# Second FFN of a two-layer decoder: the sums of x one product earlier, the third pair's products woven into the end of the first two, and another place for the shorter split distance

## The chip, the cores and the metric

One core of one Trainium2 chip runs the whole program. The metric is the device time in microseconds (us) of one execution; the comparison below goes by the median of several runs. All matrix products are done in fp32r (a 32-bit format that TensorE takes), with each operand split in two: a high part (a rounded copy, made by ScalarE) and a low part (the operand minus its high part, made by VectorE). A product of two split operands takes three matmuls: high by high, high by low, low by high.

## The reference

```python
def _swiglu(x, w_gate, w_up, w_down):
    return (jax.nn.silu(x @ w_gate) * (x @ w_up)) @ w_down

def reference(x, ...):
    for i in range(DEPTH):                       # DEPTH = 2
        if i % N_MIXERS == 0:
            h = _multiscale_pool(x, pool_w[j], pool_scale[j])
        else:
            h = _diff_attention(x, w_qkv[j], w_o[j], lam_p[j], subln_g[j], rel_table, lambda_init)
        x = _layernorm(ALPHA * x + h, ln_mix_g[i], ln_mix_b[i])
        x = _layernorm(ALPHA * x + _swiglu(x, w_gate[i], w_up[i], w_down[i]), ln_ffn_g[i], ln_ffn_b[i])
    return x
```

x is 512 tokens by 1024 features; the hidden width of the FFN is 2816. The change touches only the FFN of the second layer (i = 1), and there only its opening: the first of the products with `w_gate` and `w_up`.

## The kernel before

The program is one instruction stream per engine, in the order in which the Python code issues it; each engine works through its own list in order, and semaphores make an instruction wait for its inputs. So the place of a line in the Python loop decides what stands in front of it on its engine.

**Seven products for eight.** Gate and up products of the FFN are computed with a scheme of the Strassen kind: for each index k of 0 to 10 (a pair of hidden blocks) seven products named P1, Q5, P6, Q3, P7, P2 and Q4 replace eight. Each is a run of 24 matmuls of 128x256 (`run`, line 966). P1, P2 and Q4 multiply quarters of x itself; Q5, P6, P7 and Q3 multiply sums of quarters of x, which are kept in `xs[:, m]` with m = 0, 1, 2, 3 in that order. P1, P6, P7 of one k add up in a PSUM bank called A, P2 in B, Q4 in D, Q5 and Q3 in C. In the middle of an accumulation the bank is copied out and then added to further: after P6 of a k, ScalarE copies bank A to `first` (line 985), and P7 of the same k, which adds to bank A, has to wait for that copy. In the same way Q5 is copied out of bank C (line 983) before Q3 adds to it.

**The opening order.** In the second layer the 21 products of k = 0, 1, 2 are run in the order of the list `FIRST`. In this text product j is the one at place j in that list, and chunk j is the piece of weights that it multiplies; chunk j has the names w108 to w111 for j = 0 to 3 and g_4, g_5, ... for j = 4, 5, ... in the trace, with h and l for the high and the low part. Before the change the order is

- j = 0 to 5: P1, P2 of k = 0, 1, 2; j = 6, 7, 8: Q4 of k = 0, 1, 2
- j = 9, 10: Q5 of k = 0, 1; j = 11, 12: P6; j = 13, 14: P7; j = 15, 16: Q3 of k = 0, 1
- j = 17, 18, 19, 20: Q5, P6, P7, Q3 of k = 2.

From j = 21 on come the seven products of k = 3, then of k = 4, and so on.

**Weights.** A chunk is loaded by SyncE's queue into one of five `raw` buffers (512 KB each); the load of chunk c waits until the low part of chunk c - 5 has been made, since that frees the buffer. ScalarE casts the chunk to its high part (line 711), VectorE makes the low part (line 714). There are six pairs of split buffers. `advance(upto)` issues casts and lows until the chunks below `upto` are complete; a cast of chunk c + 1 stands ahead of the low of chunk c. `ahead(j + 6)` after product j therefore issues the cast of chunk j + 6 and the low of chunk j + 5; `ahead(j + 5)` is one chunk less. From chunk 22 on, weights of k = 3 are partly sums of raw pieces that VectorE adds (line 708).

**Sums of x.** `sums_of_x` is a generator. In the second layer it has seven steps, and the loop issues one step per product (`next(sums)`). With r0 to r3 the four quarters of x, low and high being the split of a sum into `xs`:

- step 1: r1 = r0 - r1 (line 766); step 2: high of `xs[0]`, r0 = r2 - r0 (769); step 3: low of `xs[0]`, r2 = r1 - r2 (772); step 4: high of `xs[1]`, r3 = r3 + r2 (775)
- step 5: low of `xs[1]`, high of `xs[2]`; step 6: low of `xs[2]`, high of `xs[3]`; step 7: low of `xs[3]`.

The highs are casts of 128x1024 on ScalarE (line 751), the rest is VectorE (the lows are line 754).

**What else stands in the lists.** After j = 3, 5 and 7 a gate sum (lines 1026 and 1027) copies bank A of k = 0, 1, 2 and adds bank B. After each Q4, ScalarE copies bank D (line 998). After P7, VectorE and ScalarE compute the second half of the hidden block (lines 989, 1001, 1002, 1003), after Q3 the first half (lines 987, 1017). At the same time GpSimd's queue moves weight sums through DRAM (`tsum`), with DMAs that wait only for each other.

Of the kernel before, what the change touches and what calls it, by code (L numbers as in the profile page):

```python
# [52 lines left out]
GATE = ("P1", "Q5", "P6", "Q3", "P7", "P2", "Q4")  # L53
FIRST = [(k, p) for k in range(3) for p in ("P1", "P2")]
FIRST += [(k, "Q4") for k in range(3)]
FIRST += [(k, p) for ks in ((0, 1), (2,)) for p in ("Q5", "P6", "P7", "Q3") for k in ks]
PAIRS = [(0, 2), (2, 2), (4, 2), (6, 2), (8, 2), (10, 1)]


# [1 line left out]
def trunk(ctx, tc, x, wall, pscale, lam_p, subln, table, lng, lnb, first, onehot, out):  # L61
# [6 lines left out]
    def bank(name):  # L68
        return ps.tile([P, 512], F32, tag="bank", name=name)
# [523 lines left out]
    def ffn(layer, late):  # L593
# [8 lines left out]
        with tc.tile_pool(name=f"ffn{layer}", bufs=1) as fp:  # L602
# [118 lines left out]
            def ahead(upto):  # L721
                advance(upto)
                if upto > len(chunks):
                    prepare(upto - len(chunks), upto - len(chunks))
# [181 lines left out]
            def prepare(upto, lefts):  # L906
                while prepared[0] < min(upto, len(items)):
                    refill()
                    split_item(prepared[0])
                    held[0] -= 1  # L910
                    prepared[0] += 1
                while prepared[1] < min(lefts, len(items)):
                    left(prepared[1])
                    prepared[1] += 1
# [14 lines left out]
            def strassen(k):  # L929
                first_pairs = early_sums and k < 3  # L930
# [15 lines left out]
                def both(t):  # L946
                    return t.rearrange("p (f t) -> p f t", f=2)

                def tile_of(i):
                    if first_pairs and i == 0:  # L950
                        return hid[:, (6, 7, 17)[k], :]
                    return keep.tile([P, S], F32, tag="y", name=f"sg{layer}_{k}_{i}", bufs=2)

                def run(p):
                    j = place[k, p]
                    if names[p] not in banks:
                        banks[names[p]] = bank(f"{names[p]}{layer}_{k}")
                    acc = banks[names[p]]
                    h, l = halves[j]
                    xh, xl = lefts[p]  # L960
                    for f in range(2):
                        o = acc[:, f * 256 : (f + 1) * 256]
                        for kk in range(4):
                            c = slice((4 * f + kk) * P, (4 * f + kk + 1) * P)
                            for e, (w, x) in enumerate(((h, xh), (h, xl), (l, xh))):
                                nc.tensor.matmul(  # L966
                                    o, w[:, c], x[:, kk, :],
                                    start=(p in opening and not (onto and p == "P2")) and f + kk + e == 0,
                                    stop=p in closing and (f, kk, e) == (1, 3, 2),
                                    skip_group_check=True,  # L970
                                )
                    acc = both(acc)
                    if first_pairs and p in ("P1", "P2"):
                        return
                    g1 = None
                    if p == "P1" and onto:
                        banks["B"] = bank(f"B{layer}_{k}")
                        nc.scalar.copy(banks["B"], banks["A"])
                    elif p == "P1":
                        tiles[0] = tile_of(0)  # L980
                        nc.scalar.copy(both(tiles[0]), acc)
                    elif p == "Q5":
                        nc.scalar.copy(second, acc)  # L983
                    elif p == "P6":
                        nc.scalar.copy(first, acc)  # L985
                    elif p == "Q3":
                        tt(first, acc, first, op=ALU.subtract)  # L987
                    elif p == "P7":
                        tt(second, second, acc, op=ALU.subtract)
                    elif p == "P2":  # L990
                        if not onto:
                            tt(both(tiles[0]), acc, both(tiles[0]), op=ALU.add)
                    elif not first_pairs:
                        g1 = tile_of(1)
                        nc.scalar.activation(both(g1), acc, AF.Silu)  # L995
                    elif first_pairs:
                        tiles[1] = hid[:, (18, 8, 19)[k], :]
                        nc.scalar.copy(both(tiles[1]), acc)
                    if first_pairs and p == "P7":
                        g1 = tile_of(1)  # L1000
                        tt(both(g1), acc, both(tiles[1]), op=ALU.add)
                        nc.scalar.activation(g1, g1, AF.Silu)
                        tt(second, both(g1), second, op=ALU.mult)
                    if j >= early:
                        ahead(j + (5 if first_pairs and j >= 17 else 6))
                        if not (early_sums and p == "P7"):
                            catch_up()
                        if early_sums and j > 9:
                            next(chain, None)
                    if not early_sums and k == split_pairs[0] and p == "P1":  # L1010
                        weight_sums()
                    if p == "P2":
                        if onto:
                            tiles[0] = tile_of(0)
                        nc.scalar.activation(tiles[0], banks["B"] if onto else tiles[0], AF.Silu)
                    elif p == ("Q3" if first_pairs else "Q4"):
                        tt(first, both(tiles[0]), first, op=ALU.mult)
                        if not first_pairs:
                            tt(second, both(g1), second, op=ALU.mult)
                        if not early_sums and k < HALF - 1:  # L1020
                            weight_sums()
                        (owing if early_sums else behind).append(sum_hidden(k))
# [13 lines left out]
            sums = sums_of_x()  # L1036
            if early_sums:
                for i in range(2):
                    saved[1, i] = spare(4 + 11 * i)
                chain = in_pairs([down_sums(i) for i in range(AHEAD, len(PAIRS))])  # L1040
                runs = [strassen(k) for k in range(3)]
                gate_sums_after = (3, 5, 7)
                for j, (k, p) in enumerate(FIRST):
                    runs[k][0](p)
                    if j < 2:
                        advance(5 + j, True)
                        late[0, j]()
                    if j == 1:
                        nc.scalar.preload_act_table_set("silu_and_others")
                    if 2 <= j < early:  # L1050
                        advance(j + 5, True)
                    if 2 < j < 10:
                        next(sums)
                    if j in gate_sums_after:
                        runs[gate_sums_after.index(j)][1]()
                    if p == "P6":
                        runs[k][2]()
            else:
                accs = [(bank(f"g{layer}_{f}"), bank(f"u{layer}_{f}")) for f in range(early)]
                load_terms(0)  # L1060
                load_terms(1)
                for lo in (0, 256):
                    for f in range(early):
                        for i in range(2):
                            product(accs[f][i], 2 * f + i, lo, lo + 256)
                            if not lo and (f, i) in late:
                                late[f, i]()
                            if not lo and f + i:
                                advance(6, True)
                                next(sums, None)  # L1070
                        if lo:
                            advance(2 * f + 6)
                            gated(order[f], *accs[f])
                            catch_up()
                            next(sums, None)
                            if f < 2:
                                weight_sums()
                            if f == 1:
                                behind.append(sum_hidden(0))
                plain(early)  # L1080
# [66 lines left out]
            for p in DOWN:  # L1147
# [5 lines left out]
                for i in range(together):  # L1153
                    j = j0 + i
# [652 lines left out]
```

## Time and profile before

| | us |
|---|---|
| median of 3 runs | 931.76 (931.69 to 931.82) |
| the profiled execution, its own time | 931.79 |
| its span, first to last instruction | 930.0 |
| TensorE busy (PE) | 919.2 (99%) |
| VectorE busy (DVE) | 812.1 (87%) |
| ScalarE busy (ACT) | 522.7 (56%) |
| GpSimd busy (POOL) | 151.1 (16%) |

The time of the profiled execution exceeds its span by 1.8 us, which lie around the program. PEld is the loading of weights into TensorE, which overlaps PE; SPq is SyncE's queue of DMA issues. Rows of the order-of-time view give start, duration, engine, line, operation, out<-in, shapes and count, and in brackets how long the engine was idle before and what ended that. Matmuls overlap in time: each row lasts longer than the distance to the next. All starts are microseconds from the start of the span. The opening of the second FFN runs from 591 to 656.

### The profile page before, as it was taken

The page shows a single profiled execution, that of the slowest core. Times are in us where ns is not written, and L with a number is a line of the kernel's source. Part 1 is how long each engine was busy: PE and PEld are TensorE (multiplying, and loading weights), DVE is VectorE, ACT ScalarE, POOL GpSimd, SP SyncE. Part 2 cuts the span into 40 slices and gives each one's busy share as a digit, 9 for nine tenths or more (in the row PEclk, how much of TensorE's full clock was granted, in tenths as well). Part 3 has the DMA queues.
Part 4 walks back from the last instruction along what each step waited for, and adds up shares of the span by engine and source line. Part 5 has one row for each costly group of instructions (what it writes and reads, how often), then busy time and mean ns, then how long its engine had stood idle before and what let it go on. Part 6 is the DMA issues. An engine that isn't in the chain of part 4 may idle for free.

```text
span 930.0 us, 16198 instructions
## 1 busy us (share of the span) xinstructions
PE 919.2 (99%) x6285; PEld 850.3 (91%) x6285; DVE 812.1 (87%) x1199; ACT 522.7 (56%) x849; POOL 151.1 (16%) x203
## 2 busy tenths in 40 slices
PE   9999999999999999999999999999999999999996
PEld 8999999999988888988888888999999999988885
DVE  7999999998978798788787898888899999987687
ACT  5744555554653467565556675885555544654470
POOL 2311121110001101432423233222000000001100
PEclk9999999999999999999999999999999999999998
DMA  7388898896877965998999879999344644577952
GB/s 277 120 249 268 286 282 253 264 289 193 257 241 245 374 210 165 297 265 227 272 243 244 196 247 291 271 336 302 99 140 156 207 134 137 154 252 253 372 180 90
DMA packets 77962, 217.08 MB, mean 233 GB/s; under 512 B 7732, under 2 KB 19188, under 8 KB 77342
## 3 DMA queue, kind: packets, MB, share of 16 engines
q1 hardware_dynamic: 37660, 122.16, 38.8%
q0 software_dynamic: 22576, 70.79, 30.2%
q10 hardware_dynamic: 17650, 23.10, 6.9%
q8 instruction: 49, 0.80, 0.3%
q14 instruction: 27, 0.22, 0.1%
HBM read 190.84 MB, written 67.13 MB: 277 GB/s over the span
## 4 chain that ended last, share of the span: by engine, by line
PE 89%; DVE 4%; ACT 3%; issue 1%; DMA 1%; SPq 0%; POOL 0%; DVEq 0%; POOLq 0%; ACTq 0%
PE A L966 23%; PE P L1116 16%; PE C L966 12%; PE Q L1116 6%; PE B L966 5%; PE s L1385 2%; PE v L149 2%; PE v L150 2%; PE v L151 2%; PE k L149 2%; PE k L151 2%; PE q L149 2%; PE k L150 2%; PE q L150 2%; PE q L151 2%
## 5 line engine op out<-in xcount | busy, mean ns | idle before, releaser
L708 DVE TENSOR_TENSOR raw<-raw,raw 128x1024 f32<-128x1024 f32 x68 | 83.0, 1221 | 0.9
L894 POOL DMA_DIRECT2D xs<-ssum x24 | 17.3, 720 | 290.2 <-DVE d_14l L125 199.5
L124 ACT CAST xs<-hid 128x512 fp32r<-128x512 f32 (+1 forms) x60 | 34.6, 582 | 25.3 <-DVE hid L902 25.3
L301 POOL DMA_DIRECT2D tsum<-in_wall x44 | 39.5, 1305 | 42.8 <-DMA tsum<-in_wall 24.0
L125 DVE TENSOR_TENSOR xs<-hid,xs 128x512 fp32r<-128x512 f32 (+1 forms) x60 | 38.5, 644 | 7.8 <-ACT xs L124 7.8
L1395 ACT ACTIVATE p<-p,mn 128x128 f32<-128x128 f32 (+3 forms) x64 | 35.4, 554 | 12.9 <-DVE mn L1390 12.9
L1390 DVE CUSTOM_DVE_ANT_0 p<-s,bias 128x128 f32<-128x128 f32 (+3 forms) x64 | 28.1, 486 | 0.0
L987 DVE TENSOR_TENSOR hid<-C,hid 128x512 f32<-128x512 f32 x20 | 13.8, 690 | 13.8 <-PE C L966 12.4
L270 ACT ACTIVATE y<-pt,gbT 128x128 f32<-128x128 f32 x56 | 21.0, 457 | 6.3 <-PE pt L242 6.2
L858 ACT CAST v<-u 128x512 fp32r<-128x512 f32 x22 | 13.6, 620 | 18.3 <-DVE u L856 18.2
L983 ACT COPY hid<-C 128x512 f32<-128x512 f32 x20 | 11.7, 586 | 21.6 <-PE C L966 21.6
L187 DVE BATCH_NORM_STATS2 st<-res 128x6 f32<-128x512 f32 x32 | 22.2, 695 | 1.1
L301 POOL DMA_DIRECT2D gsum<-in_wall x24 | 20.2, 1278 | 13.9 <-DMA gsum<-gsum 7.1
L821 POOL DMA_DIRECT2D b<-in_wall x12 | 9.0, 795 | 83.1 <-DMA tsum<-b 54.8
L125 DVE TENSOR_TENSOR heads<-k,heads 128x512 fp32r<-128x512 f32 x8 | 5.5, 693 | 16.8 <-ACT heads L124 16.8
L1409 DVE SCALAR_TENSOR_TENSOR p<-p,sm,p 128x128 f32<-128x128 f32 (+3 forms) x32 | 17.7, 552 | 1.1
L995 ACT ACTIVATE sg<-A 128x512 f32<-128x512 f32 x17 | 10.1, 595 | 14.8 <-PE A L966 14.8
L985 ACT COPY hid<-A 128x512 f32<-128x512 f32 x20 | 11.7, 586 | 11.9 <-PE A L966 10.6
L124 ACT CAST heads<-k 128x512 fp32r<-128x512 f32 x8 | 4.7, 587 | 23.9 <-PE k L151 23.9
L1385 PE MATMUL s<-heads 64*128 64x256 f32 (+2 forms) x192 | 17.9, 330 | 0.0
L1103 DVE SCALAR_TENSOR_TENSOR res<-res,P 128x512 f32<-128x512 f32 x20 | 13.3, 682 | 4.9 <-PE P L1116 4.9
L125 POOL TENSOR_TENSOR sql<-sq,sqh 128x512 fp32r<-128x512 f32 x7 | 9.0, 1287 | 50.2 <-ACT sqh L124 50.2
(1496 smaller groups left out, 3789.1 us busy)
## 6 DMA issues: line engine op xcount, KB each, us to landing
raw<-in_wall SPq DMA_DIRECT2D x116, 512.0 KB, 5.5
r<-tsum SPq DMA_DIRECT2D x40, 512.0 KB, 4.3
r<-in_wall SPq DMA_DIRECT2D x30, 512.0 KB, 4.8
tsum<-in_wall POOLq DMA_DIRECT2D x46, 256.0 KB, 9.4
ssum<-v ACTq DMA_DIRECT2D x22, 512.0 KB, 3.6
xs<-ssum POOLq DMA_DIRECT2D x20, 512.0 KB, 7.7
b<-in_wall POOLq DMA_DIRECT2D x18, 512.0 KB, 5.9
hid<-in_wall POOLq DMA_DIRECT2D x15, 512.0 KB, 5.8
```

The lines of the kernel that those rows point to most:

```text
L124: nc.scalar.copy(dst_h, src)
L125: (low or nc.vector).tensor_tensor(dst_l, src, dst_h.bitcast(F32), op=ALU.subtract)
L149: nc.tensor.matmul(acc, ah, bh, start=start, stop=False)
L150: nc.tensor.matmul(acc, ah, bl, start=False, stop=False)
L151: nc.tensor.matmul(acc, al, bh, start=False, stop=stop)
L301: nc.gpsimd.dma_start(out=dst[:, c], in_=src[:, c], accum_op=ALU.add)
L708: tt(t, raws[pair[0]], raws[pair[1]], op=ALU.add)
L966: nc.tensor.matmul(o, w[:, c], x[:, kk, :], start=(p in opening and not (onto and p == "P2")) and f + kk + e == 0, stop=p in closing and ( ...
L1116: nc.tensor.matmul(accs[s], x[:, k, r], y[:, c], start=first and k == 0 and e == 0, stop=last and k == m - 1 and e == 2, skip_group_check= ...
L1385: nc.tensor.matmul(accs[c][:, :wide], a[r, qs], b[r, :wide], start=i == 0, stop=i == 2)
L1390: nc.vector.tensor_tensor_reduce(out=p, in0=accs[c][:, :w], in1=biases[h][:, w - 1 :: -1] if w < S else biases[h][:, ::-1], op0=ALU.add, o ...
L1395: nc.scalar.activation(p, p, AF.Exp, bias=mn[:, q, c : c + 1], scale=-1.0, accum_out=sm[:, q, c : c + 1],)
```

## The change

Three edits, all in the second layer:

1. The list `FIRST`: Q3 of k = 1 moves back by two places, so that j = 15 is Q3 of k = 0, j = 16 is Q5 of k = 2, j = 17 is P6 of k = 2, j = 18 is Q3 of k = 1; j = 19 and 20 stay P7 and Q3 of k = 2. The chunks and their loads follow the same list.
2. The steps of the sums of x are issued after j = 2 to 8 instead of j = 3 to 9, and after j = 2 to 5 they stand ahead of the split of the next chunk instead of behind it.
3. `ahead(j + 5)` instead of `ahead(j + 6)` applies from j = 19 on instead of from j = 17 on (to j = 20).

```diff
@@ -53,7 +53,8 @@
 GATE = ("P1", "Q5", "P6", "Q3", "P7", "P2", "Q4")
 FIRST = [(k, p) for k in range(3) for p in ("P1", "P2")]
 FIRST += [(k, "Q4") for k in range(3)]
-FIRST += [(k, p) for ks in ((0, 1), (2,)) for p in ("Q5", "P6", "P7", "Q3") for k in ks]
+FIRST += [(k, p) for p in ("Q5", "P6", "P7") for k in range(2)]
+FIRST += [(0, "Q3"), (2, "Q5"), (2, "P6"), (1, "Q3"), (2, "P7"), (2, "Q3")]
 PAIRS = [(0, 2), (2, 2), (4, 2), (6, 2), (8, 2), (10, 1)]
@@ -1002,7 +1003,7 @@
                     if j >= early:
-                        ahead(j + (5 if first_pairs and j >= 17 else 6))
+                        ahead(j + (5 if first_pairs and j >= 19 else 6))
                         if not (early_sums and p == "P7"):
                             catch_up()
@@ -1047,10 +1048,10 @@
                         late[0, j]()
                     if j == 1:
                         nc.scalar.preload_act_table_set("silu_and_others")
+                    if 1 < j < 9:
+                        next(sums)
                     if 2 <= j < early:
                         advance(j + 5, True)
-                    if 2 < j < 10:
-                        next(sums)
                     if j in gate_sums_after:
                         runs[gate_sums_after.index(j)][1]()
```

## The prediction

> **What bounds the kernel now.** I read the busy times of the page first, then who keeps PE waiting, then PE, ACT, DVE and the load queue in order of time.
>
> ```profile
> span 930.0 us, 16198 instructions
> PE 919.2 (99%) x6285; PEld 850.3 (91%) x6285; DVE 812.1 (87%) x1199; ACT 522.7 (56%) x849; POOL 151.1 (16%) x203
> PE A L966 <- ACT hid L985: 1.3, 2, 0.7
> PE pool L412 <- DVE still L356: 1.1, 1, 1.1
> PE A L966 <- DVE xs L754: 0.2, 1, 0.2
> 618.90:655.70 36.80, 35.34 (x290) 34.73 (x289) 31.14 (x35) 23.58 (x31) 6.60 (x9) 1.00 0.92 283
> 655.70:797.00 141.30, 141.30 (x1178) 141.22 (x1177) 134.28 (x160) 73.21 (x93) 0.00 (x0) 1.00 0.46 146
> ```
>
> PE is the bound, 99% of the span. In the whole execution three groups of waits stand against it (third to fifth row: in total, times, longest); the one on L412 is in the first layer. The other groups, two waits and one, lie in the stretch that the change edits. The last two rows, two stretches (length, then busy time of PE, PEld, DVE, ACT, POOL, then the granted clock) say the same: in products 9 to 20 PE has idle time, while from 655.7 on it is busy throughout. So what the change can win is what stands between these products:
>
> ```profile
> 621.82 0.40 PE L966 MATMUL C<-xs,g_10h 128*128 128x256 f32 x2
> 624.70 0.28 PE L966 MATMUL A<-xs,g_11h 128*128 128x256 f32 x1
> 625.15 0.39 PE L966 MATMUL A<-xs,g_11h 128*128 128x256 f32 x1 [0.18 <-DVE xs L754]
> 630.77 0.28 PE L966 MATMUL A<-xs,g_12l 128*128 128x256 f32 x1
> 631.66 0.50 PE L966 MATMUL A<-xs,g_13h 128*128 128x256 f32 x2 [0.61 <-ACT hid L985]
> 648.91 0.28 PE L966 MATMUL A<-xs,g_18l 128*128 128x256 f32 x1
> 649.86 0.50 PE L966 MATMUL A<-xs,g_19h 128*128 128x256 f32 x2 [0.68 <-ACT hid L985]
> 655.72 0.40 PE L966 MATMUL A<-xt,g_21h 128*128 128x256 f32 x2
> ```
>
> An undisturbed product takes 624.70 - 621.82 = 2.88 us, 0.12 per matmul. Against that pace there are three holes. Product 11 (P6 of k = 0) issues its first matmul at 624.70 and its second at 625.15 instead of 624.82: 0.33. Product 13 (P7 of k = 0) should follow at 630.77 + 0.12 = 630.89 and starts at 631.66: 0.77. Product 19 (P7 of k = 2) should follow at 649.03 and starts at 649.86: 0.83. The idle figures in brackets are smaller, since a matmul's row runs on past the issue of the next. The first matmuls after a hole are slower as well: the row at 649.86 lasts 0.50 for two in place of 0.40. Product 11 starts at 624.70 and product 21 at 655.72: 31.02 for ten products that need 28.8. So 2.2 us is all there is in holes: 0.24% of the time.
>
> **The change part by part.** The number of matmuls, casts, subtractions and DMAs stays the same; only places in the lists move.
>
> *Weaving (edit 1).* The hole at 649.86 is P6 directly followed by P7 of the same k: the copy out of bank A stands between them.
>
> ```profile
> 649.22 0.59 ACT L985 COPY hid<-A 128x512 f32<-128x512 f32 x1 [2.29 <-PE A L966]
> 641.35 1.04 ACT L711 CAST g_21h<-raw 128x1024 fp32r<-128x1024 f32 x1
> ```
>
> ACT had been idle for 2.29 us and started as soon as P6 was done, so nothing but the order can shorten this. In the new order product 18 (Q3 of k = 1) lies between them: 2.88 us of PE work for a copy of 0.59, which finds ACT free, as its list is empty after the cast that starts at 641.35. The hole goes, with its slow start: 0.83 + 0.10 = **-0.93 us**. What Q3 itself needs is made well ahead by the same lists: `xs[:, 3]` by steps 6 and 7, after products 7 and 8; chunk 18 after products 12 and 13.
>
> *Sums one product earlier (edit 2).* The first hole ends with the low of `xs[:, 1]`:
>
> ```profile
> 606.69 0.69 DVE L125 TENSOR_TENSOR xt<-hid,xt 128x512 fp32r<-128x512 f32 x1 [1.37 <-ACT xt L124]
> 609.05 1.23 DVE L714 TENSOR_TENSOR g_6l<-raw,g_6h 128x1024 fp32r<-128x1024 f32 x1 [1.67 <-ACT g_6h L711]
> 610.19 1.22 DVE L714 TENSOR_TENSOR g_7l<-raw,g_7h 128x1024 fp32r<-128x1024 f32 x1
> 611.33 1.22 DVE L766 TENSOR_TENSOR hid<-hid 128x1024 f32<-128x1024 f32 x1
> 620.47 1.22 DVE L714 TENSOR_TENSOR g_11l<-raw,g_11h 128x1024 fp32r<-128x1024 f32 x1
> 621.60 1.22 DVE L775 TENSOR_TENSOR saved<-saved 128x1024 f32<-128x1024 f32 x1
> 623.87 1.23 DVE L754 TENSOR_TENSOR xs<-saved,xs 128x1024 fp32r<-128x1024 f32 x1
> ```
>
> DVE is idle for 1.67 us before 609.05, then works without a break; 1.14 us per large operation. In the new order step 1 (L766) stands ahead of the low of chunk 6 and fits into that idle time: about 607.3 to 608.5. From 609.05 to the end of the low of chunk 11 DVE had twelve operations. It still has twelve, since L766 goes out and L775 (step 4) comes in ahead. So the low of chunk 11 ends at 621.7 as before. Directly behind it now stands the low of `xs[:, 1]`, from 621.7 to 622.9 instead of 623.87 to 625.10, ahead of product 11's second matmul at 624.82. The first hole goes by itself: 0.33 + 0.10 = 0.43.
>
> Its price is paid on ACT. The high of `xs[:, 1]` now stands ahead of the cast of chunk 9 and waits for L772, which comes sixth from 609.05: four large operations and one of 0.60 ahead of it, start about 614.2, end 615.4. The cast of chunk 6 ends at 609.0 (its low follows at once); behind it ACT has a cast of `xs`, the casts of chunks 7 and 8 and a copy, at 0.95 and 0.48 each, and is through by 612.3. So it stands for 3 us with the casts of chunks 9 and 10 queued behind. From 615.4 on ACT runs that high, the cast of chunk 9 and two copies, the second of which frees bank D of k = 0, at about 618.4; DVE has the low of chunk 8, L775 and the low of chunk 9, which ends at about 618.8. Product 9 starts two products of 2.88 ahead of 624.70, at 618.93, and needs the low 0.24 later. That holds with 0.3 us to spare, and if it fails by as much again, the second hole, below, swallows it.
>
> *The second hole.* Here I expect little. Product 13 waits for L985, the copy after P6 of k = 0. ACT was late with it:
>
> ```profile
> 623.24 1.05 ACT L711 CAST g_13h<-raw 128x1024 fp32r<-128x1024 f32 x1 [0.40 <-DMA raw<-gsum]
> 626.26 1.05 ACT L711 CAST g_14h<-raw 128x1024 fp32r<-128x1024 f32 x1
> 627.22 1.05 ACT L751 CAST xs<-saved 128x1024 fp32r<-128x1024 f32 x1
> 628.17 0.58 ACT L983 COPY hid<-C 128x512 f32<-128x512 f32 x1
> 628.64 1.05 ACT L711 CAST g_15h<-raw 128x1024 fp32r<-128x1024 f32 x1
> 629.59 0.59 ACT L983 COPY hid<-C 128x512 f32<-128x512 f32 x1
> 630.07 1.05 ACT L711 CAST g_16h<-raw 128x1024 fp32r<-128x1024 f32 x1
> 631.02 0.59 ACT L985 COPY hid<-A 128x512 f32<-128x512 f32 x1
> L107 SPq DMA_DIRECT2D raw<-gsum x1: 319/319/319, 616.6 to 616.6; - x1
> DMA to landing us min/median/max: 9.6/9.6/9.6
> L107 SPq DMA_DIRECT2D raw<-in_wall x1: 332/332/332, 621.7 to 621.7; - x1
> DMA to landing us min/median/max: 8.2/8.2/8.2
> ```
>
> The cast at 627.22 (step 6, high of `xs[:, 3]`) moves ahead of 626.26, into the time in which ACT waits for chunk 14, whose load (first pair of the last four rows) was issued at 616.6 and landed 9.6 later, at 626.2. Everything behind moves up by one cast, 0.95 us: C copy 627.2, cast of chunk 15 627.7, C copy 628.6, and ACT is ready for chunk 16 at 629.1. But chunk 16 (last pair) is issued at 621.7, when the low of chunk 11 is done, and lands at 621.7 + 8.2 = 629.9. The new order doesn't bring that issue forward. So its cast starts at 629.9 to 630.0 instead of 630.07, L985 starts at 630.9 and ends at 631.5, and product 13 starts at 631.55 instead of 631.66: **-0.1 us**. The 0.43 of the first hole is no gain on top: PE reaches product 13 earlier (630.5) and waits there for 1.1 us instead of 0.77. What is late next, after the sums, is the load.
>
> *Loads that are issued later.* The lows of chunks 7, 8 and 9 have sums ahead of them now: one more large operation in front of chunk 7, two in front of chunks 8 and 9. So the loads of chunks 12, 13 and 14 are issued 1.1, 2.3 and 2.3 us later; those of 15 and 16 at the old time. I cost this at nothing as long as each of these loads reaches the queue while the one before it is still under way: chunk 14's at 618.9, while chunk 13 lands just ahead of its cast at 623.24: a margin of 4 us. Bounds for chunk 16's landing: not under 629.1 to any use (ACT isn't there before), and not over 632.1, if chunk 14 kept its 9.6 us from issue to landing and 16 its distance of 3.7 behind it. I take 629.9, since chunk 16's own issue stays.
>
> *Shorter distance later (edit 3).* After product 17 three casts (22, 24, 25), two sums and one low are issued one product earlier; after product 18 the same for chunk 23. With six split buffers the cast of chunk 25 has to wait for the end of product 18, about 648.8. Behind it on ACT stand the silu of k = 2 and the cast of chunk 23. The silu is used after product 20 ends at 654.6, chunk 23 by PE from 660 on. DVE's list is not blocked by that cast. Zero, covered by two products; without that cover it would cost the length of a cast, 1.05. That SyncE's refills for k = 4 can go earlier, and three loads swap places, is free in the same way. POOL's queue gets nothing past it: its DMAs wait for each other.
>
> **The sum:** -0.93 - 0.1 = -1.03 us. The profiled execution took 931.79 (1.8 around its span of 930.0), 0.03 over the median of 931.76; from the median, **930.7**. What this kernel's runs can tell from no change is about 0.2%, 1.86 us; the forecast is inside that.
>
> **Rivals.** *Full recovery.* Chunk 16 lands by 629.1, so ACT alone sets product 13: L985 at 630.1, product 13 at 630.7, -0.95 in place of -0.1, and -1.9 in all: 929.9. For it: the load took 8.2 us because it shared the DMA engines, and POOL's share may fall otherwise. Against: its issue stays, and up to 630 the queues have the same bytes to move. With all three holes gone without rest it would be 929.55, the floor.
>
> *The loads run dry (slower).* Place: the loads of chunks 13 and 14, issued 2.3 us later, leave SyncE's queue without work at some engines, and POOL's transfers take over.
>
> ```profile
> q0 software_dynamic: 581, 1.35, 57.4%
> q1 hardware_dynamic: 551, 2.05, 49.6%
> ```
>
> These are the shares of POOL's (q0) and SyncE's queue (q1) from 613 to 624: both have work, and the engines are full. At the upper bound chunk 16 lands at 632.1, product 13 starts at 633.8, +2.1 against before, -0.93 for the weave: 932.9. It turns into a loss from the point where chunk 16 lands 1.0 us late. Against it: the margin of 4 us. The Trainium skill, DMA: Bandwidth & Descriptors, Queues, rings and completion order, says that each DMA engine takes turns between the queues that have work for it, packet by packet; by that a queue that has run dry loses its turns to the other, and the time would be nearer to 932.9. By that same rule a queue that is never dry keeps its half, and the near-equal shares above agree with that; then the sum stays at 930.7.
>
> *The weave doesn't do what it says.* ACT reaches the copy of P6 of k = 2 late, because casts that wait for buffers stand ahead. Then the hole stays: 931.65. Against: that list is empty from 642.4 on.
>
> **How the numbers follow.** Forecast 0.68, with its own range of 930.3 to 931.0 (chunk 16 by 0.3 either way). Full recovery 0.14, loads dry 0.10, no weave 0.05, other 0.03. The range reaches to full recovery below and to the first half of the dry case above: 929.8 to 931.6. Faster by over 0.2% needs more than -1.86, which full recovery just reaches: 0.11. Slower by over 0.2% lies beyond the bound of the dry case: 0.04. Within: 0.85.
>
> **What would show it.** Product 18 is Q3 of k = 1, and product 19 follows without idle time. Product 11 has no wait for `xs`. L766 stands ahead of the low of chunk 6, ACT waits for some 3 us before the high of `xs[:, 1]`. Product 13 still waits on L985 for about 1 us, and ACT in front of the cast of chunk 16 on its load. Product 21 starts at about 654.7, and all behind it keeps its distances. Wrong would be: a wait of product 9 of over 1 us, chunk 16 landing outside of 629.6 to 630.3, or a new wait of PE behind 655.

## The result, and the profile after

| | before | changed |
|---|---|---|
| median, us | 931.74 (20 runs) | 930.66 (20 runs) |
| lowest to highest | 931.02 to 935.03 | 929.27 to 932.12 |
| ratio, 95% interval | | 0.9985 [0.9979, 0.9992] |
| profiled execution, its own time | 931.79 | 929.88 |

The kernel is 1.08 us faster by the medians, whose ratio is 0.9988; 930.7 had been forecast, a gain of 1.03. The ratio in the table isn't that of the medians; by it the gain is 1.4 us. Its interval lies clear of 1, and the gain is inside 0.2% either way.

Of the changed kernel, first the page:

```profile
span 928.1 us, 16198 instructions
PE 918.4 (99%) x6285; PEld 850.2 (92%) x6285; DVE 811.9 (87%) x1199; ACT 523.1 (56%) x849; POOL 151.7 (16%) x203
```

the waits of PE over the whole execution (in total, times, longest):

```profile
PE pool L413 <- DVE still L357: 1.1, 1, 1.1
PE A L967 <- ACT hid L986: 0.3, 1, 0.3
PE D L967 <- DVE g_8l L715: 0.2, 1, 0.2
PE pt L243 <- DVE tbl L540: 0.2, 1, 0.2
```

and the stretches of products 9 to 20 and of what follows, cut just ahead of the same products as before (length, then busy time of PE first and the granted clock third from the end):

```profile
618.60:653.70 35.10, 34.81 (x291) 34.60 (x290) 31.02 (x33) 24.12 (x32) 6.62 (x9) 1.00 0.95 298
653.70:795.00 141.30, 141.30 (x1178) 141.22 (x1177) 132.82 (x159) 72.81 (x93) 0.00 (x0) 1.00 0.44 146
```

In the first stretch PE's idle time falls from 1.46 us to 0.29. Line numbers are one higher, since the list takes a line more. The waits at L413 and L243 lie ahead of the FFN, in the first 40 us. Of the waits on the copy of P6 (L985 before, L986 now) one of two is left and shorter, the wait for `xs` is gone, and a wait of product 8 for the low part of its chunk has come. In order of time on PE:

```profile
590.43 0.40 PE L967 MATMUL A<-xt,w108h 128*128 128x256 f32 x2
615.39 0.40 PE L967 MATMUL D<-xt,g_8h 128*128 128x256 f32 x2
615.95 0.39 PE L967 MATMUL D<-xt,g_8l 128*128 128x256 f32 x1 [0.16 <-DVE g_8l L715]
630.08 0.28 PE L967 MATMUL A<-xs,g_12l 128*128 128x256 f32 x1
630.65 0.50 PE L967 MATMUL A<-xs,g_13h 128*128 128x256 f32 x2 [0.29 <-ACT hid L986]
647.90 0.28 PE L967 MATMUL C<-xs,g_18l 128*128 128x256 f32 x1
648.02 0.40 PE L967 MATMUL A<-xs,g_19h 128*128 128x256 f32 x2
653.78 0.40 PE L967 MATMUL A<-xt,g_21h 128*128 128x256 f32 x2
```

Product 19 follows 0.12 us after the last matmul of product 18: the weave's hole is gone. Product 8 issues the matmul with its low part 0.32 late, product 13 starts 0.45 late (630.65 against 630.08 + 0.12).

One yardstick serves for all that follows: the time from the first matmul of product 0 to the first of product 21. After it is 653.78 - 590.43 = 63.35. Before it was 64.63, as product 0 started at 591.09:

```profile
591.09 0.28 PE L966 MATMUL A<-xt,w108h 128*128 128x256 f32 x1
```

So the opening gained 1.28 us in these two executions. The spans differ by 1.9; the other 0.66 lies ahead of product 0, where the change does nothing. In the profiles below product 0 starts anywhere from 589.5 to 591.5. What follows product 21 takes 274.3 in both.

### The profile page after: what moved, and what is told of

The parts are those of the page before. It is cut to its first block, busy times and chain, and to the rows that moved or that the text cites. A ratio compares the mean times of both kernels' runs of the same rounds, so it can differ in the third digit from the quotient of the medians.

```text
span 928.1 us, 16198 instructions
## 1 busy us (share of the span) xinstructions
PE 918.4 (99%) x6285; PEld 850.2 (92%) x6285; DVE 811.9 (87%) x1199; ACT 523.1 (56%) x849; POOL 151.7 (16%) x203
## 3 DMA queue, kind: packets, MB, share of 16 engines
q1 hardware_dynamic: 37660, 122.16, 38.8%
## 4 chain that ended last, share of the span: by engine, by line
PE 90%; ACT 4%; DVE 4%; issue 1%; DMA 1%; POOL 0%; DVEq 0%; ACTq 0%; POOLq 0%
PE A L967 22%; PE P L1117 16%; PE C L967 12%; PE Q L1117 6%; PE B L967 5%; PE s L1386 2%; PE v L150 2%; PE v L152 2%; PE v L151 2%; PE k L150 2%; PE k L152 2%; PE q L150 2%; PE k L151 2%; PE q L151 2%; PE q L152 2%
## 5 line engine op out<-in xcount | busy, mean ns | idle before, releaser
L302 POOL DMA_DIRECT2D tsum<-in_wall x44 | 38.8, 1291 | 42.7 <-DMA tsum<-in_wall 22.6
L986 ACT COPY hid<-A 128x512 f32<-128x512 f32 x20 | 11.8, 589 | 12.7 <-PE A L967 11.5
```

Of the source, the lines that this page charges most:

```text
L302: nc.gpsimd.dma_start(out=dst[:, c], in_=src[:, c], accum_op=ALU.add)
```

## The experiments

Each time was taken beside runs of the kernel before on the same chip. Their medians were 931.74 for the changed kernel, 932.09 for weave, sums, firststep and latecast, 931.91 for again, nodist, hold and both, and 931.78 for distonly and bothhold. The ratios in the table differ from those of the medians by up to 0.0006, which is 0.6 us. "Opening" is the yardstick and "product 13" how much later than at an undisturbed pace it starts, both in us and from the one profiled execution of each kernel.

| kernel | median, us | ratio to before, 95% | opening | product 13 |
|---|---|---|---|---|
| before | | | 64.63 | 0.77 |
| changed | 930.66 | 0.9985 [0.9979, 0.9992] | 63.35 | 0.45 |
| again | 930.41 | 0.9985 [0.9974, 0.9996] | 63.92 | 1.01 |
| weave | 931.87 | 0.9999 [0.9990, 1.0008] | 64.84 | 1.79 |
| sums | 932.22 | 1.0001 [0.9991, 1.0011] | 65.45 | 1.62 |
| distonly | 934.97 | 1.0035 [1.0022, 1.0047] | 68.63 | 1.39 |
| nodist | 931.83 | 0.9998 [0.9988, 1.0009] | 64.24 | 1.35 |
| firststep | 931.15 | 0.9990 [0.9981, 0.9999] | 63.75 | 1.23 |
| latecast | 929.64 | 0.9976 [0.9966, 0.9986] | 63.02 | 0.11 |
| hold | 929.64 | 0.9973 [0.9963, 0.9983] | 62.76 | 0 |
| both | 929.73 | 0.9971 [0.9961, 0.9981] | 62.41 | 0 |
| bothhold | 929.10 | 0.9977 [0.9967, 0.9987] | 62.36 | 0 |

**weave: edit 1 alone.**

```diff
-FIRST += [(k, p) for ks in ((0, 1), (2,)) for p in ("Q5", "P6", "P7", "Q3") for k in ks]
+FIRST += [(k, p) for p in ("Q5", "P6", "P7") for k in range(2)]
+FIRST += [(0, "Q3"), (2, "Q5"), (2, "P6"), (1, "Q3"), (2, "P7"), (2, "Q3")]
```

> The woven order of products alone; sums of x and split distance as before. From the start of product 0 to the start of product 21 the kernel before takes 64.63 us and the changed kernel 63.35, of which the 12 undisturbed products and the turns of rows 2 and 3 set 62.47. Theory (three separate holes; the weave removes the one ahead of product 19 and nothing else): the holes ahead of products 11 (0.43) and 13 (0.87) stay, 64.63 - 0.93 = 63.7, time 930.8, ratio 0.9990. Rival 1 (the weave does it all, the earlier sums bring nothing): 63.35, time 930.45. Rival 2 (the weave also needs the longer distance, and makes a new wait at product 22 or 23 without it): above 63.7.

No gain. The hole ahead of product 19 is gone, but a new one of 0.96 us has come ahead of product 24, behind product 21, so the opening doesn't hold it. Rival 2 has the right idea and the wrong product. Besides, the hole ahead of product 13 was 1.0 us longer than in the profile of before, with the same order of instructions up to there.

**sums: edit 2 alone.**

```diff
+                    if 1 < j < 9:
+                        next(sums)
                     if 2 <= j < early:
                         advance(j + 5, True)
-                    if 2 < j < 10:
-                        next(sums)
```

> The sums of x one product earlier alone; order of products and distance as before. Theory: the hole ahead of product 11 goes, the one ahead of product 13 shrinks by about 0.4, a new one of 0.4 comes at product 8 (low part of chunk 8 behind two operations of the sums), the one ahead of product 19 stays: 63.35 + 0.93 = 64.28, so -0.35 us, ratio 0.9996. Rival (the second hole is set by the load of chunk 16 and does not move): -0.1, 64.5. Rival (the earlier sums bring as much as the weave): 63.7.

Three of the four holes are as expected: no wait at product 11, 0.32 at product 8, 0.83 at product 19. The fourth isn't: the hole ahead of product 13 was to shrink by 0.4 and grew from 0.77 to 1.62. Chunk 13's load was issued at the same time as in the changed kernel, but its cast started 34.07 after product 0, where the changed kernel's started at 32.90. By the times there is no gain. No run has the weave and edit 3 with the sums in their old place, so what the earlier sums add to those two isn't shown.

**distonly: edit 3 alone.**

```diff
-                        ahead(j + (5 if first_pairs and j >= 17 else 6))
+                        ahead(j + (5 if first_pairs and j >= 19 else 6))
```

> The third edit alone: order of products and place of the sums as before, distance 6 until product 18. Theory (edit 3 is needed only by the woven order, whose undoing cost 1.1 us ahead of product 24): nothing gained in the old order; the holes ahead of products 11, 13 and 19 stay, none comes at 24, time of before, ratio 1.000. Rival (the longer distance gains 1 us in the old order too): product 21 or what follows it 1 us earlier, ratio 0.999.

Both theories fell: it costs 3.2 us. On ACT:

```profile
648.21 1.05 ACT L711 CAST g_22h<-raw 128x1024 fp32r<-128x1024 f32 x1 [1.33 <-DVE raw L708]
649.17 1.04 ACT L711 CAST g_24h<-raw 128x1024 fp32r<-128x1024 f32 x1
650.11 1.04 ACT L711 CAST g_25h<-raw 128x1024 fp32r<-128x1024 f32 x1
651.06 0.57 ACT L985 COPY hid<-A 128x512 f32<-128x512 f32 x1
```

In the old order the longer distance puts the three casts of k = 3 right ahead of the copy after P6 of k = 2, for which product 19 waits. By the profile of before, where it starts 0.31 after the start of the last row of P6, the copy was due at about 649.2; it starts at 651.06. The hole on PE is 2.7 us, and then the clock halves. PE in order of time:

```profile
648.86 0.28 PE L966 MATMUL A<-xs,g_18l 128*128 128x256 f32 x1
651.69 0.50 PE L966 MATMUL A<-xs,g_19h 128*128 128x256 f32 x2 [2.55 <-ACT hid L985]
```

and stretches ahead of it and behind it, with the granted clock as the third figure from the end:

```profile
645.00:649.00 4.00, 4.00 (x35) 3.93 (x33) 3.97 (x5) 1.38 (x2) 1.27 (x2) 1.00 0.92 233
652.50:655.70 3.20, 3.20 (x17) 3.20 (x16) 0.42 (x1) 0.00 (x0) 0.00 (x0) 0.50 0.52 172
658.00:661.00 3.00, 3.00 (x27) 3.00 (x27) 2.30 (x4) 0.63 (x1) 0.00 (x0) 1.00 0.00 0
```

**nodist: the changed kernel with edit 3 undone** (`j >= 17` again).

> The changed kernel with its third edit undone: distance 5 from product 17 on, as before. In the run with the weave alone a new hole of 1.0 us stood ahead of product 24 (Q3 of k = 3), behind the copy of bank C. Theory (the woven order needs the later switch: with the short distance the casts of k = 3 come one product later and meet the silu and the copies of k = 2 on ScalarE): the hole ahead of product 24 is there, 1.0 to 1.1 us, and nothing else differs from the changed kernel; time 931.7. Rival (that hole belongs to the late sums of x, or to the 1 us by which that run was late): no hole, 930.66.

The theory held for product 24. The hole of 0.96 us is there, with a slow start behind it, and the gain is gone (0.9998). That nothing else would differ didn't hold: product 13 was later too, by 0.9 against the changed kernel, with the same order of instructions up to there. On PE, then on ACT, then on DVE:

```profile
662.85 0.28 PE L967 MATMUL A<-xs,g_23l 128*128 128x256 f32 x1
663.93 0.50 PE L967 MATMUL C<-xs,g_24h 128*128 128x256 f32 x2 [0.80 <-ACT hid L984]
650.69 1.05 ACT L712 CAST g_22h<-raw 128x1024 fp32r<-128x1024 f32 x1 [3.67 <-DVE raw L709]
662.35 1.05 ACT L712 CAST g_27h<-raw 128x1024 fp32r<-128x1024 f32 x1 [2.38 <-DVE raw L709]
663.31 0.58 ACT L984 COPY hid<-C 128x512 f32<-128x512 f32 x1
648.78 0.69 DVE L988 TENSOR_TENSOR hid<-C,hid 128x512 f32<-128x512 f32 x1 [2.61 <-PE C L967]
649.38 2.47 DVE L709 TENSOR_TENSOR raw<-raw,raw 128x1024 f32<-128x1024 f32 x2
661.05 1.22 DVE L709 TENSOR_TENSOR raw<-raw,raw 128x1024 f32<-128x1024 f32 x1
```

In the woven order the sums of k = 3's weights stand behind the subtraction after Q3 of k = 1 on DVE if they are issued after product 18. DVE stands for 2.61 us until Q3 is done, and ACT for 3.67 us until the first sum is. After product 0 the first sums start 4.1 us later than in the changed kernel, and the sum for chunk 27, at 661.05, still 3.6 later; the copy of bank C that product 24 needs stands behind the cast of that chunk. In the changed kernel this copy starts 69.65 us after product 0, here 73.21. So the weave and edit 3 are one edit: each alone brings nothing or a loss.

**firststep: only step 1 ahead of the split.**

```diff
-                    if 1 < j < 9:
+                    if j == 2:
                         next(sums)
                     if 2 <= j < early:
                         advance(j + 5, True)
+                    if 2 < j < 9:
+                        next(sums)
```

> The changed kernel, but only step 1 of the sums of x stands ahead of the split of the next chunk; steps 2 to 7 come one product early but behind that split. So the lows of chunks 7 and 8 have no sums ahead of them any more, that of chunk 9 one less, and the loads of chunks 12 and 13 are issued 1.1 and 2.3 us earlier again. Theory (the hole at product 8 is the two operations ahead of the low of chunk 8; the hole ahead of product 13 is a list of ScalarE that starts with the landing of chunk 13, which the later issue made 1.0 us later): no wait at product 8, chunk 13 lands at about 31.8 after the start of product 0 instead of 32.8, the copy of P6 of k = 0 starts at 39.2 instead of 39.56, product 21 at 63.0 instead of 63.35; time 930.3. Rival 1 (the later issue of the loads costs nothing, chunk 16's own load sets that copy): copy at 39.56 as before, 63.35, since the 0.41 of product 8 is swallowed by a longer wait at product 13. Rival 2 (the place of the sums ahead of the split is what brings the gain): 63.8.

Product 8 doesn't wait, as expected, and chunk 13's cast starts at 32.2 after product 0 in place of 32.9 (about 31.8 had been expected). But the copy after P6 came at 39.97, not 39.2, for another load:

```profile
626.65 1.05 ACT L712 CAST g_14h<-raw 128x1024 fp32r<-128x1024 f32 x1
627.61 0.58 ACT L984 COPY hid<-C 128x512 f32<-128x512 f32 x1
628.60 1.05 ACT L712 CAST g_15h<-raw 128x1024 fp32r<-128x1024 f32 x1 [0.41 <-DMA raw<-in_wall]
629.55 0.58 ACT L984 COPY hid<-C 128x512 f32<-128x512 f32 x1
630.47 1.05 ACT L712 CAST g_16h<-raw 128x1024 fp32r<-128x1024 f32 x1 [0.34 <-DMA raw<-gsum]
631.42 0.58 ACT L986 COPY hid<-A 128x512 f32<-128x512 f32 x1
```

ACT waits for chunk 15, then for chunk 16, and only then makes the copy: here rival 1 has it, though the copy is 0.4 later than it said. So bringing chunk 13 forward didn't shorten the hole. The 0.41 won at product 8 went into the longer wait at product 13.

**latecast: the cast of chunk 16 behind the copy.**

```diff
-                        ahead(j + (5 if first_pairs and j >= 19 else 6))
+                        ahead(j + (5 if first_pairs and (j >= 19 or 10 <= j < 12) else 6))
```

> The changed kernel with the distance of splits at 5 instead of 6 also after products 10 and 11, so that the cast of chunk 16 stands behind the copy of P6 of k = 0 on ScalarE and the cast of chunk 17 behind that of k = 1. Theory (product 13 waits for that copy, and the copy for the cast that stands ahead of it): the copy starts one cast earlier, at about 38.6 after the start of product 0, ends at 39.2, product 13 would be reached at 39.77; no wait there, product 21 at 62.9 instead of 63.35, time 930.2. Rival 1 (the copy is late for what stands further ahead, the landing of chunk 13 or 14): under half of that, 63.15 or more. Rival 2 (shorter distance makes chunk 16 or 17 late for product 16 or 17): a new wait there, 63.4 or more.

The theory held in kind: product 13 is 0.1 late, the median 2.4 us below before. The copy started at 39.23 after product 0, not at 38.6, as ACT waited 0.32 for chunk 15. This run also shows that the cast ahead of the copy was the matter, not the load as such (first ACT, then PE):

```profile
629.96 0.58 ACT L984 COPY hid<-C 128x512 f32<-128x512 f32 x1
630.44 0.59 ACT L986 COPY hid<-A 128x512 f32<-128x512 f32 x1
631.73 1.05 ACT L712 CAST g_16h<-raw 128x1024 fp32r<-128x1024 f32 x1 [0.70 <-DMA raw<-gsum]
630.85 0.28 PE L967 MATMUL A<-xs,g_12l 128*128 128x256 f32 x1
631.08 0.39 PE L967 MATMUL A<-xs,g_13h 128*128 128x256 f32 x1
```

Chunk 16 came later than in any of the other profiles, and its cast waited, but behind the copy, where it disturbs nobody.

**hold: GpSimd's last weight sums held back until about 645** (the kernel is otherwise the changed one, and nothing is left out).

```diff
-                chain = in_pairs([down_sums(i) for i in range(AHEAD, len(PAIRS))])
+                gate = keep.tile([P, 1], F32R, name="gate")
+                def held_sums():
+                    yield from in_pairs([down_sums(i) for i in (2, 3)])
+                    l = halves[21][1][:, :1].bitcast(F32)
+                    nc.gpsimd.tensor_tensor(gate, l, l, op=ALU.subtract)
+                    yield from in_pairs([down_sums(i) for i in (4, 5)])
+                chain = held_sums()
```

> The changed kernel with GpSimd's weight sums of the last two pairs of down chunks (the DMAs on GpSimd's queue from 603 to 650 us) held back until the low of chunk 21 is made, at about 645. Nothing is left out. Theory (what makes the hole ahead of product 13, and lets it vary from run to run, is the sharing of the DMA engines: chunks 13 to 16 land 7 to 8 us after their issue, where loads alone take 4 to 5): chunk 13 lands at about 30.5 after the start of product 0 instead of 32.8, the copy of P6 of k = 0 ends by 38.8, no hole ahead of product 13, product 21 at 62.9 instead of 63.35, and the times spread less than the 929.3 to 932.1 of the changed kernel; median 930.2 or less. Rival (the copy is late by ScalarE's own list, whatever the loads do): hole of 0.45 as before, 63.35. Rival (the held transfers collide with the loads behind 645): a new wait behind product 21, no gain.

No hole ahead of product 13, though ACT's list is that of the changed kernel. The times spread over 1.3 us (929.22 to 930.53, 8 runs) in place of 2.9 (20 runs); with so few runs, and with product 0 itself starting up to 2 us apart in the profiles, a smaller spread isn't shown. From issue to landing, the loads of chunks 12, 13, 14 and 16 (the trace has no landing for 15; shortest, median, longest) took in the changed kernel

```profile
DMA to landing us min/median/max: 7.3/7.5/8.0
```

and in this one

```profile
DMA to landing us min/median/max: 3.3/3.4/4.6
```

**both: the edits of firststep and latecast together.**

> The changed kernel with both edits that were run singly: only step 1 of the sums ahead of the split, and distance 5 after products 10 and 11. Theory (the wait at product 8 is the order of the low of chunk 8, the one at product 13 the casts ahead of the copy, and the two are independent): neither is there, product 21 starts 62.5 us after product 0 (63.35 in the changed kernel, 63.02 with the shorter distance alone); time 929.3. Rival (the wait at product 8 costs nothing, since the copy of P6 sets product 13 all the same): 63.0, time 929.7.

No wait of PE is left in the opening: 62.41 us, 929.73. The interval overlaps those of latecast and hold, so that the wait at product 8 is worth its 0.4 us is shown by the opening, not by the times.

**again: the changed kernel once more.**

> The changed kernel once more, unchanged, beside the others. Theory (the hole ahead of product 13 follows the landing of chunks 13 to 16, which differ by 1 us and more from one execution to the next): product 8 waits 0.3 to 0.4 us again, product 13 by another amount than 0.46, between 0.1 and 1.8; product 19 and 24 not at all; time 930.66 within 0.7. Rival (the hole has a fixed size): 0.46 within 0.1.

Product 8 waits 0.32 as before, product 13 1.01 in place of 0.45. ACT waited 0.74 us for chunk 13 and 0.32 for chunk 15, but not for 16. So this hole has no fixed size. The nodist kernel has the same order of instructions up to product 17 and makes a third case: 1.35.

**bothhold: both, and the sums held.**

> The changed kernel with step 1 alone ahead of the split, distance 5 after products 10 and 11, and GpSimd's last weight sums held back until the low of chunk 21. Theory (with the first two no hole is left between products 0 and 21, so the third can only take away the spread of the times): product 21 at 62.4 after product 0 as with the first two alone, median 929.5 within 0.3, range of runs under 1.5. Rival (the held transfers free the loads further ahead or cost something behind): 0.3 or more to either side.

929.10, the lowest median (though not the lowest ratio), its opening as expected. But the spread wasn't as small as that of hold (928.59 to 930.55), and behind product 21 it took 274.8 in place of 274.3, 0.3 of it in a new wait of product 30. Whether it is better than both isn't settled by the intervals.

## Why the prediction was right or wrong

**The sum** of -1.03 met a measured -1.08, and the range held. That it came so near is in part luck. The sum is nearly all weave, and the weave stands as a gain only together with edit 3. The other term, -0.1 at product 13, is smaller than the difference between two executions of one order: after product 0, product 13 started at 40.57 and 41.21 in the old order (before, distonly) and at 40.22, 40.78 and 41.11 in the new one (changed, again, nodist); 40.46 had been forecast. So no run confirms or refutes that term.

*The weave, -0.93: the hole was read rightly, but the term doesn't stand alone.* The hole ahead of product 19 is gone. But the prediction put -0.93 down to edit 1 and zero to edit 3, "covered by two products". That zero is the step of the prediction that failed: it looked at what the later switch might cost and not at what leaving it out would. Nodist and weave show that without edit 3 the woven order pays 0.96 us and a slow start at product 24, and distonly that edit 3 without the weave costs 3.2 us. The rival of the weave that fails (casts ahead of the copy) is just what distonly shows, in the old order.

*Sums earlier, the first hole and its price: right, with one place missed.* Product 11 doesn't wait. DVE and ACT did what was worked out (in order of time, first DVE, then ACT):

```profile
606.76 1.23 DVE L767 TENSOR_TENSOR hid<-hid 128x1024 f32<-128x1024 f32 x1
614.68 1.22 DVE L715 TENSOR_TENSOR g_8l<-raw,g_8h 128x1024 fp32r<-128x1024 f32 x1
619.88 1.22 DVE L715 TENSOR_TENSOR g_11l<-raw,g_11h 128x1024 fp32r<-128x1024 f32 x1
```

```profile
614.79 1.05 ACT L752 CAST xs<-saved 128x1024 fp32r<-128x1024 f32 x1 [3.10 <-DVE saved L773]
```

Step 1 went into the idle time, ACT stood for 3.10 us, and the low of chunk 11 ended at 621.10, which is 30.67 after product 0 against 30.60 before. What failed here was to test the margin at product 9 alone. The low of chunk 8, with two sums in front of it, ends at 615.90; product 8 wants it at 615.63. By the same sum as for chunk 9 it could have been seen: from 609.05, five large operations and one of 0.60 ahead of it, it would end at about 616.6, while product 8, at 616.05 before, wants it 0.24 later. The 0.41 that this costs is swallowed at product 13, as the 0.43 of the first hole was to be.

*The second hole, -0.1: right kind, and a size that isn't one number.* Product 13 still waits on the copy after P6, by 0.45 in the profile of the changed kernel and 1.01 in the next; the forecast was 1.1. In the first, chunk 16 landed 7.5 us after its issue in place of 8.2, and its cast didn't wait. That is 38.2 after product 0 where 38.8 had been forecast, and outside of the bounds (629.6 to 630.3, or 38.5 to 39.2 after product 0) that the prediction itself gave as a sign of being wrong; in the next profile it landed at 38.9, inside of them. In neither did ACT wait for it, as the prediction had said it would. In the first profile the start of ACT's list was chunk 13:

```profile
623.33 1.05 ACT L712 CAST g_13h<-raw 128x1024 fp32r<-128x1024 f32 x1 [0.82 <-DMA raw<-gsum]
629.03 1.08 ACT L712 CAST g_16h<-raw 128x1024 fp32r<-128x1024 f32 x1
629.99 0.61 ACT L986 COPY hid<-A 128x512 f32<-128x512 f32 x1
```

From 623.33 ACT has no idle time up to the copy: five large casts at 0.95 and four copies at 0.48 make 6.7 us. So the loads that are issued later, which the prediction cost at nothing, aren't free in this profile: chunk 13, issued 2.3 us later, landed 32.8 after product 0 against 31.8 before. How much of the hole that makes isn't shown, as firststep brought chunk 13 forward and kept the hole. In firststep chunk 16 was the last wait ahead of the copy, as forecast, with one for chunk 15 ahead of that. Hold and latecast each take the hole away, all or nearly all of it: with GpSimd's transfers out of the way the loads take less than half the time, and the hole is gone with ACT's order as it was; with the cast of chunk 16 behind the copy it shrinks to 0.1 with the loads as slow as ever. So in the changed kernel the hole needs both, the slow loads and the cast ahead of the copy.

*The rivals.* Full recovery was priced at -1.9 and took place in neither profile of the changed kernel, although in the first chunk 16 landed within 0.2 us of the time that this rival asks for; its floor (all holes gone, 929.55) is about what the kernel both reached, 929.73. Loads dry would have had chunk 16 up to 2.2 us late; in the first profile it was 0.6 early, and only chunk 13 was late, by 1.0. Chunk 14's load was issued 5 us before that of chunk 13 landed (4 had been worked out), so that the queue ran dry isn't shown. The turns that queues take by the Trainium skill (DMA: Bandwidth & Descriptors, Queues, rings and completion order), cited there, fit hold: SyncE's loads take 3.4 us alone and 7.5 beside GpSimd's. No run shows the turns themselves.

## What to carry to other kernels

An order of work written by hand is a list per engine, so a product moved on one engine moves the place of what the others issue behind it: price such edits together, and test the deadline of each product whose split gets something ahead of it, not only of the last one. Where a copy that the bound engine waits for stands behind a cast that waits for a load, put the copy first; in latecast and both that took away the wait, or all but 0.1 us of it, with the load as late as before or later. A hole whose end hangs on transfers beside those of another queue differed by up to 0.9 us here from one execution to the next, so give it a range from several profiles.

## What had not been expected of the hardware

A hole of 2.7 us on PE in distonly was followed by over 3 us at half the granted clock, which cost another 1.6 us (product 19 took 4.46 in place of 2.88, 0.1 of it the slow start seen behind the other holes too); holes of up to 1.8 us (weave, 1.79) left the clock at full. Where between the two the limit lies isn't shown. And the same order of instructions and loads (before and distonly are alike up to product 17) gave holes of 0.77 and 1.39 us ahead of product 13, with nothing on ACT but the landing of loads between them: chunk 16 landed 38.8 us after product 0 in one and 39.5 in the other, and only in the other did its cast wait.
